# Hybrid DeltaNet/MLA trunk on one core: three products give [channel, token], and the stream's norm acts after the products that read it

## Chip, cores and metric

One NeuronCore of a Trainium2 chip runs the whole program. The metric is device time in microseconds (us) of one execution; lower is better.

## What is computed (the reference, cut)

A residual stream of 16 meta tokens and 1024 tokens, 1024 channels, goes through one gated-DeltaNet layer (A) and one multi-head latent attention layer (B). All is float32.

```python
o = gated_delta_rule(q, k, v, g, beta)               # A, 8 heads of 128
o = rms_norm(o, o_gain) * silu(gate)                 # per head
x = x + o @ w_out                                    # A's output projection
h = rms_norm(x, kv_norm);  c = h @ w_down            # 1024 -> 256 + 64
c_kv = rms_norm(c[..., :256], g_latent);  k_pe = c[..., 256:]
h = rms_norm(x, b_norm);  z = h @ w_in               # 1024 -> 384 + 1024
c_q = rms_norm(z[..., :384], g_q_latent);  gate = z[..., 384:]
o = attention(c_q, c_kv, k_pe) * silu(gate)
out = x + o @ w_out                                  # B's output projection, meta tokens dropped
```

## The kernel before, in words

Every float32 product is made of three F32R products, high by high, high by low and low by high (`mm3`, L92 to L95), so one 128x128 weight block costs three matmuls, each with its own weight load. A product over 1024 channels is 8 blocks (`kt`), 24 matmuls into one PSUM bank. The order of instructions on each engine is set by a scheduler at build time from the program's order, its pools and their buffer counts; at run time each engine works in that order and waits on semaphores. All loads and stores of the stages below are issued by SyncE (SP), one after the other.

Stages around the change, in time order. Tokens stand in chunks TOKC of 272, 384 and 384 columns, or in tiles (16 meta tokens, t = -1, and eight of 128).

- Gates of A (L739 to L754): per head three products of 24 matmuls, [channel, token], Silu on ScalarE (ACT). Gate 7 stays in SBUF as `glast`.
- Output projection of A (L758 to L853). `out_gather` loads a tile of o, scales it by the heads' norms (VectorE, L766), turns it with 8 transposes (L776), multiplies by the gate and splits it into oTh and oTl. `out_project` multiplies: oT is stationary, 512 columns of the weight move, twice 24 matmuls for a tile, result [token, channel]. The residual is added (L824), the row stored to x1_scr; Square with a running sum and an rsqrt give the norm, GpSimd (POOL) scales the row (xs, L830), and `turn` transposes it again (8 per tile, L840) into h1_hi and h1_lo, which are [channel, token] and normalised.
- Latents (L864 to L970): per tile 24 matmuls of 320 columns for the key side and 24 of 384 for the query side, [token, channel]; norms per row, then transposes (L940, L958) and a split into ckvT and cqT.
- Gate of B: per head 2 x 24 matmuls of 512 columns, and ACT takes Silu straight from PSUM (L84, called there). Then attention.
- Output projection of B (`out_b`): per tile a load of oT (512 KB), a cast and a subtraction, a load of x1, 2 x 24 matmuls of 512 columns (wf), an addition, one store of 512 KB.

PSUM banks in these stages have three names: sc (5 banks, products), bd (2, transposes and small products) and pt (1).

Of the kernel before, what the change touches and what calls it, by code (L numbers as in the profile page):

```python
# [121 lines left out]
def body(ctx: ExitStack, tc: tile.TileContext, I, out):  # L122
# [63 lines left out]
    with ExitStack() as la:  # L186
        hp = la.enter_context(tpool(name="hT", bufs=1, side="right"))
        wp = la.enter_context(tpool(name="wA", bufs=2, side="right"))
        zp = la.enter_context(tpool(name="zA", bufs=2, side="right"))
# [547 lines left out]
        with ExitStack() as lr:  # L737
            rp = lr.enter_context(tpool(name="wr", bufs=2))
            for h in range(H):  # L739
                hi, lo = weights(3 * D + h * P)  # L740
                z = zp.tile([P, 3 + L], F32, tag="z", name=nm("zg"))[:, 0:L] if h < HG else glast[:, h - HG, :]
                for c, (a, b) in enumerate(TOKC):
                    act(z[:, a:b], gemm_T(hi, lo, c), AF.Silu)
                if h < HG:
                    SY.dma_start(gt_scr[h * P:(h + 1) * P, :], z)
                raw = rp.tile([P, D], F32, tag="raw", name=nm("raw"))
                SY.dma_start(raw, I["a_w_out"][0, h * P:(h + 1) * P, :])
                last = split_w(raw, w_hi[:, h, :], w_lo[:, h, :], col("og"), A)
                if h > 1:
                    next(norms, None)  # L750
            for _ in norms:
                pass
            with tc.issue_after(last.ins):
                refine_norms()  # L754
# [751 lines left out]
```

## Time and profile before

| | |
|---|---|
| median of 3 runs | 1332.45 us (1331.79 to 1336.11) |
| profiled execution: time, span | 1339.67 us, 1338.0 us |
| TensorE (PE) busy | 1301.6 us, 97% of the span |
| VectorE (DVE), ScalarE (ACT), GpSimd (POOL) busy | 67%, 43%, 24% |
| mean granted TensorE clock | 0.986 |

The times come from a profile of one execution; its span is the time from the first to the last instruction. Busy times of matmuls overlap one another, since they are pipelined, so the price of a matmul is read from the distance of two starts in a row, not from its duration.

### The profile page before, as it was taken

What the parts mean: (1) busy time and instruction counts of PE and PEld (TensorE: products, weight loads), DVE (VectorE), ACT (ScalarE), POOL (GpSimd) and SP (SyncE); (2) the same over time, 40 slices, a digit from 0 to 9 for tenths busy, and PEclk for the clock granted to TensorE, in tenths of its full rate; (3) what the DMA queues carried; (4) which work ended last, traced back from release to release, by engine and by line L of the source; (5) the groups of instructions that cost most, each with busy time, mean ns of one, the idle gap of its engine ahead of it and who ended that gap; (6) DMA issues with size and microseconds to landing.
All of it is one profiled execution on the core that took longest, in us unless ns stands there. A gap on an engine that the chain in (4) does not pass through costs nothing.

```text
span 1338.0 us, 24787 instructions
## 1 busy us (share of the span) xinstructions
PE 1301.6 (97%) x9047; PEld 1181.1 (88%) x9047; DVE 893.4 (67%) x2588; ACT 581.4 (43%) x1760; POOL 327.2 (24%) x597
## 2 busy tenths in 40 slices
PE   6999999999999999999999999997999999998998
PEld 4889989989998999997887798886999999998886
DVE  7679779878976894652553855225888888787321
ACT  6543444344424431232132342116777777776200
POOL 3141121122111100040111402212534535447000
PEclk9999999999998999999999999999999999999999
DMA  5111112111111203164441303211101101014443
GB/s 195 32 34 49 49 30 60 36 41 42 54 48 31 58 27 97 60 229 134 154 134 66 94 1 112 95 48 61 55 25 40 51 25 33 22 36 147 137 142 110
DMA packets 91676, 96.80 MB, mean 72 GB/s; under 512 B 27423, under 2 KB 72415, under 8 KB 91555
## 3 DMA queue, kind: packets, MB, share of 16 engines
q1 hardware_dynamic: 91554, 95.23, 22.8%
q8 instruction: 71, 1.16, 0.4%
q14 instruction: 51, 0.41, 0.1%
HBM read 68.19 MB, written 27.01 MB: 71 GB/s over the span
## 4 chain that ended last, share of the span: by engine, by line
PE 83%; DVE 6%; ACT 3%; issue 3%; POOL 2%; DMA 1%; SPq 0%; DVEq 0%; POOLq 0%; ACTq 0%
PE mm L93 9%; PE mm L94 9%; PE mm L95 9%; PE sc L95 6%; PE sc L94 6%; PE sc L93 6%; PE bd L93 5%; PE bd L95 4%; PE bd L94 4%; PE pt L1336 2%; PE tr L507 2%; PE ch L639 1%; PE tr L499 1%; PE ch L649 1%; PE ch L635 1%
## 5 line engine op out<-in xcount | busy, mean ns | idle before, releaser
L93 PE MATMUL mm<-hT_hi,whi 128*128 128x384 f32 (+1 forms) x768 | 257.2, 335 | 4.3 <-ACT hT_hi L292 4.3
L94 PE MATMUL mm<-hT_lo,whi 128*128 128x384 f32 (+1 forms) x768 | 256.4, 334 | 0.5 <-DVE hT_lo L293 0.5
L95 PE MATMUL mm<-hT_hi,wlo 128*128 128x384 f32 (+1 forms) x768 | 255.9, 333 | 0.0
L93 PEld LDWEIGHTS mm<-hT_hi,whi 128*128 128x128 f32 x768 | 147.7, 192 | 6.3 <-POOL wab L100 5.0
L94 PEld LDWEIGHTS mm<-hT_lo,whi 128*128 128x128 f32 x768 | 147.7, 192 | 2.2 <-DVE hT_lo L293 1.0
L95 PEld LDWEIGHTS mm<-hT_hi,wlo 128*128 128x128 f32 x768 | 148.1, 193 | 1.1 <-issue 0.4
L100 POOL TENSOR_SCALAR whi<-raw 128x512 fp32r<-128x512 f32 x48 | 34.4, 733 | 171.4 <-PE mm L94 136.7
L113 DVE TENSOR_TENSOR pTl<-pt,pTh 128x256 fp32r<-128x256 f32 (+2 forms) x112 | 54.9, 494 | 10.2 <-ACT pTh L112 8.8
L395 ACT COPY z<-mm 128x384 f32<-128x384 f32 (+1 forms) x72 | 32.0, 445 | 65.4 <-PE mm L95 64.4
L84 ACT ACTIVATE P<-P,mx 128x144 f32<-128x144 f32 (+3 forms) x64 | 50.6, 791 | 21.9 <-DVE mx L1294 19.1
L93 PE MATMUL sc<-wo_hi,oTh 128*128 128x512 f32 (+1 forms) x144 | 57.5, 399 | 1.1 <-DVE oTl L783 1.1
L95 PE MATMUL sc<-wo_hi,oTl 128*128 128x512 f32 (+1 forms) x144 | 57.2, 397 | 0.0
L94 PE MATMUL sc<-wo_lo,oTh 128*128 128x512 f32 (+1 forms) x144 | 56.9, 395 | 0.0
L399 DVE SCALAR_TENSOR_TENSOR kn<-z,pcol,kn 128x384 f32<-128x384 f32 (+1 forms) x72 | 41.5, 576 | 22.9 <-ACT kn L397 22.1
L112 ACT CAST pTh<-pt 128x256 fp32r<-128x256 f32 (+2 forms) x112 | 47.3, 427 | 15.7 <-PE pt L1336 8.6
L101 DVE TENSOR_TENSOR wlo<-raw,whi 128x512 fp32r<-128x512 f32 x64 | 46.8, 741 | 8.4 <-POOL whi L100 8.3
L95 PE MATMUL sc<-h_hi,wlo 128*128 128x512 f32 x128 | 50.8, 397 | 0.0
L94 PE MATMUL sc<-h_lo,whi 128*128 128x512 f32 x128 | 50.6, 396 | 0.0
L1307 POOL TENSOR_SCALAR P<-P,sl 128x144 f32<-128x144 f32 (+3 forms) x64 | 49.7, 778 | 3.8
L93 PE MATMUL sc<-h_hi,whi 128*128 128x512 f32 x128 | 50.5, 395 | 0.0
L93 PE MATMUL sc<-kn_hi,qn_hi 128*128 128x272 f32 (+3 forms) x160 | 48.5, 305 | 2.0 <-DVE mx L1294 1.5
L107 DVE SCALAR_TENSOR_TENSOR wlo<-raw,pcol,whi 128x128 fp32r<-128x128 f32 x64 | 23.4, 429 | 39.9 <-POOL whi L106 39.9
(390 smaller groups left out, 3900.3 us busy)
## 6 DMA issues: line engine op xcount, KB each, us to landing
raw<-in_a_w_in SPq DMA_DIRECT2D x64, 256.0 KB
xt<-in_x SPq DMA_DIRECT2D x14, 512.0 KB
o_scr<-o SPq DMA_DIRECT2D x64, 64.0 KB
raw<-in_a_w_out SPq DMA_DIRECT2D x8, 512.0 KB
on<-o_scr SPq DMA_DIRECT2D x8, 512.0 KB
x_scr<-xt SPq DMA_DIRECT2D x8, 512.0 KB
raw<-in_b_w_in SPq DMA_DIRECT2D x8, 512.0 KB
gb_scr<-z SPq DMA_DIRECT2D x8, 512.0 KB
```

The source lines that it names most:

```text
L84: i = A.activation(out_ap, in_ap, func, **kw)
L93: TE.matmul(ps, ahi, bhi, start=first, stop=False)
L94: TE.matmul(ps, ahi, blo, start=False, stop=False)
L95: TE.matmul(ps, alo, bhi, start=False, stop=last)
L100: eng.tensor_scalar(out=hi, in0=raw, scalar1=1.0, scalar2=1.0, op0=ALU.mult, op1=ALU.mult)
L101: V.tensor_tensor(out=lo, in0=raw, in1=hi, op=ALU.subtract)
L112: A.copy(hi, ps)
L113: V.tensor_tensor(out=lo, in0=ps, in1=hi, op=ALU.subtract)
L395: A.copy(z[:, 3 + a:3 + b], gemm_T(hi, lo, c))
L399: V.scalar_tensor_tensor(out=yc, in0=z[:, a + j:b + j], scalar=col("cw", 24 * j + m), in1=yc, op0=ALU.mult, op1=ALU.add)
L507: TE.matmul(ps[:, P * j:P * j + P], kn[:, a:b], qT[:, a:b], start=True, stop=True)
L1307: G.tensor_scalar(out=Pm[:, 0:n], in0=Pm[:, 0:n], scalar1=s, scalar2=1.0, op0=ALU.mult, op1=ALU.mult)
```

## The change

Three products now have weights as the stationary operand and tokens as the moving one, so that their results come as [channel, token].

- A's output projection goes by chunks of tokens: 8 channel blocks of 24 matmuls for each chunk. The residual comes from x_r, a turned copy of the input; x1_scr holds [channel, token]. The sum is copied (ACT) and subtracted (DVE) straight into h1_hi and h1_lo, unnormalised; ACT squares it and DVE sums the squares over blocks into ssx. L830's scaling and `turn` are gone.
- `out_gather` scales by the heads' norms with 8 ACT multiplications in place of one on DVE. The gathers of tiles -1, 0 and 1 stand between the chunks of gate 7, the others between the channel blocks of chunks 0 and 1.
- Latents go by chunks: 3 blocks for the keys (128, 128, 64 rows) and 3 for the queries, left in PSUM until a norm is there. Norms come as rows repeated over all partitions: a float32 product with `ones` (L1009, L1039) sums squares over channels, then Ln, Exp and a step of refinement. The stream's norm is added into the latents' norms (vrow); where no norm follows it multiplies (rrow): the rotary keys and the gate of B, whose Silu then reads SBUF.
- B's output projection goes by chunks of 256, 512 and 256 tokens with 8 blocks each, loads and stores of 128 or 256 KB per block, and gives [channel, token]; the host turns the result.

The core of the diff (the functions of before stand above):

```diff
-    x1_scr = dram("x1_scr", [L, D])
+    x1_scr = dram("x1_scr", [D, L])
...
+        def out_gather(t, bank, oT_hi, oT_lo):
 
-            oT_hi = so.tile([P, KT, P], F32R, tag="oTh", name=nm("oTh"))
-            oT_lo = so.tile([P, KT, P], F32R, tag="oTl", name=nm("oTl"))
+            on, gtile = rows.pop(t)
+            for h in range(H):
+                x = on[:k, h * P:(h + 1) * P]
+                A.mul(x, x, ro[:k, s, h:h + 1])
...
-                A.copy(oT_hi[:, hs4, 0:k], gs)
-                V.tensor_tensor(out=oT_lo[:, hs4, 0:k], in0=gs, in1=oT_hi[:, hs4, 0:k], op=ALU.subtract)
-            return oT_hi, oT_lo
-        gathered = {t: out_gather(t, bank) for t in (-1, 0)}
+                A.copy(oT_hi[:, hs4], gs)
+                V.tensor_tensor(out=oT_lo[:, hs4], in0=gs, in1=oT_hi[:, hs4], op=ALU.subtract)
+        def gate(h, between=()):
+            hi, lo = weights(3 * D + h * P)
+            z = zp.tile([P, 3 + L], F32, tag="z", name=nm("zg"))[:, 0:L] if h < HG else glast[:, h - HG, :]
+            for c, (a, b) in enumerate(TOKC):
+                act(z[:, a:b], gemm_T(hi, lo, c), AF.Silu)
+                for f in between[c:c + 1]:
+                    f()
+            if h < HG:
...
+        gate(HG)
+        so = so_.enter_context(tpool(name="so", bufs=3))
+        W0 = TOKC[0][1]
+        oT0 = [so.tile([P, KT, W0], F32R, tag=y, name=y, bufs=1) for y in ("oT0h", "oT0l")]
+        def first_gather(t):
+            a, b = tok(t)
+            return lambda: out_gather(t, bank, *(x[:, :, a:b] for x in oT0))
+        for t in (-1, 0, 1):
+            gather_rows(t, so)
+        gate(H - 1, [first_gather(t) for t in (-1, 0, 1)])
...
+        def out_project(c, m, oT):
+            a, b = TOKC[c]
+            n = b - a
+            for k in range(m if m else 0, min(m + 2, KT - 1) + 1):
+                if (c, k) not in xts:
+                    load_xt(c, k)
+            xt = xts.pop((c, m))
+            ps = bank2("mm", [P, 512])[:, 0:n]
+            ms = slice(m * P, (m + 1) * P)
+            for kt in range(KT):
+                mm3(ps, w_hi[:, kt, ms], w_lo[:, kt, ms], oT[0][:, kt], oT[1][:, kt], kt == 0, kt == KT - 1)
+            V.tensor_tensor(out=xt, in0=ps, in1=xt, op=ALU.add)
+            SY.dma_start(x1_scr[ms, a:b], xt)
+            A.copy(h1_hi[:, m, a:b], xt)
+            V.tensor_tensor(out=h1_lo[:, m, a:b], in0=xt, in1=h1_hi[:, m, a:b], op=ALU.subtract)
+            if m == 0:
+                act(ssx[:, a:b], xt, AF.Square)
+            else:
+                sq = pools["x"].tile([P, n], F32, tag="sq", name=nm("sq"))
+                act(sq, xt, AF.Square)
+                V.tensor_tensor(out=ssx[:, a:b], in0=sq, in1=ssx[:, a:b], op=ALU.add)
...
+        oT = oT0
+        for c, (a, b) in enumerate(TOKC):
+            if c == 1:
+                so_.close()
+                last = so_.enter_context(tpool(name="so3", bufs=1))
+                pools["x"] = so_.enter_context(tpool(name="xo2", bufs=2))
+                oTl = [last.tile([P, KT, 384], F32R, name=y) for y in ("oTlh", "oTll")]
+            if c == 0:
+                nxt = [x[:, :, TOKC[2][0]:TOKC[2][1]] for x in (h1_hi, h1_lo)]
+            elif c == 1:
+                nxt = oTl
+            else:
+                lg_.close()
+                rrow = lpre.enter_context(tpool(name="rows", bufs=1, side="right")).tile([P, L], F32, name="rrow")
+                wdp = lwd.enter_context(tpool(name="wd", bufs=1, side="right"))
+                wd_hi, wd_lo = (wdp.tile([P, KT, WD], F32R, name=x) for x in ("wd_hi", "wd_lo"))
+                nxt = None
...
+                    t = 3 * c + 2 + m // 2
+                    x = slice(P * (m // 2), P * (m // 2 + 1))
+                    out_gather(t, bank2, *(y[:, :, x] for y in nxt))
+                    if t + 2 < NT:
+                        gather_rows(t + 2, sg)
+                if nxt is None:
+                    split_w(wdr[m], wd_hi[:, m, :], wd_lo[:, m, :], col("kv", m))
+                    if m + 2 < KT:
+                        fetch_wd(m + 2)
+            oT = nxt
...
+            def root(out_ap, put):
+                n = out_ap.shape[-1]
+                sh, t = (sp.tile([P, 384], F32, tag=x, name=nm(x), bufs=1)[:, 0:n] for x in ("rsh", "rt"))
+                y = out_ap
+                put(sh)
+                act(y, sh, AF.Ln, scale=-2.0)
+                act(y, y, AF.Exp, scale=-0.5)
+                V.tensor_tensor(out=t, in0=y, in1=y, op=ALU.mult)
+                V.tensor_tensor(out=t, in0=t, in1=sh, op=ALU.mult)
+                V.scalar_tensor_tensor(out=out_ap, in0=t, scalar=1.5, in1=y, op0=ALU.add, op1=ALU.mult)
+            def stream_norms(c):
+                a, b = TOKC[c]
+                ps = bank2("tb", [P, 512])[:, 0:b - a]
+                TE.matmul(ps, ones, ssx[:, a:b], start=True, stop=True)
+                V.tensor_scalar(out=vrow[:, a:b], in0=ps, scalar1=-0.5 * EPS / D, scalar2=-0.5 * EPS * EPS,
+                                op0=ALU.mult, op1=ALU.add)
+                root(rrow[:, a:b], lambda sh: V.tensor_scalar(
+                    out=sh, in0=ps, scalar1=-0.5 / D, scalar2=-0.5 * EPS, op0=ALU.mult, op1=ALU.add))
+            def block(hi, lo, m, k, a, b):
+                ps = bank2("mm", [P, 512])[0:k, 0:b - a]
+                ms = slice(m * P, m * P + k)
+                for kt in range(KT):
+                    mm3(ps, hi[:, kt, ms], lo[:, kt, ms], h1_hi[:, kt, a:b], h1_lo[:, kt, a:b],
                         kt == 0, kt == KT - 1)
...
+            def normalise(blocks, ss, a, b, width, hi, lo, to, gain):
+                n = b - a
+                ps = bank2("tb", [P, 512])[:, 0:n]
+                TE.matmul(ps, ones, ss, start=True, stop=True)
+                row = sp.tile([P, 384], F32, tag="row", name=nm("row"))[:, 0:n]
+                root(row, lambda sh: V.scalar_tensor_tensor(
+                    out=sh, in0=ps, scalar=-0.5 / width, in1=vrow[:, a:b], op0=ALU.mult, op1=ALU.add))
+                for j, x in enumerate(blocks):
+                    y = sp.tile([P, 384], F32, tag="nb", name=nm("nb"))[:, 0:n]
+                    V.tensor_tensor(out=y, in0=x, in1=row, op=ALU.mult)
+                    g = col(gain, j)
+                    A.mul(hi[:, j, to:to + n], y, g)
+                    V.scalar_tensor_tensor(out=lo[:, j, to:to + n], in0=y, scalar=g, in1=hi[:, j, to:to + n],
+                                           op0=ALU.mult, op1=ALU.subtract)
...
+            def latent_kv(c):
+                a, b = TOKC[c]
+                kvs, ss = [], None
                 for j in range(2):
...
+                    kvs.append(block(wd_hi, wd_lo, j, P, a, b))
+                    for _ in range(2 * c):
+                        next(wqs, None)
+                    ss = squares(kvs[j], ss)
+                    soon()
+                later.append(lambda: normalise(kvs, ss, a, b, KVR, ckvT_hi, ckvT_lo, a, "gl"))
+                if c + 1 < len(TOKC):
+                    later.append(lambda: stream_norms(c + 1))
+                ps = block(wd_hi, wd_lo, 2, ROPE, a, b)
+                for _ in range(2):
+                    next(wqs, None)
+                kp = sp.tile([ROPE, 384], F32, tag="kp", name=nm("kp"), bufs=1)[:, 0:b - a]
+                V.tensor_tensor(out=kp, in0=ps, in1=rrow[0:ROPE, a:b], op=ALU.mult)
+                soon()
+                if c == 0:
+                    later.append(all_tables)
+                later.append(lambda: rotary(c, kp))
+            def latent_q(c):
+                a, b = TOKC[c]
+                a = max(a, NM)
+                qs, ss = [], None
                 for j in range(3):
...
+                    qs.append(block(wq_hi, wq_lo, j, P, a, b))
+                    ss = squares(qs[j], ss)
+                    soon()
+                later.append(lambda: normalise(qs, ss, a, b, QR, cqT_hi, cqT_lo, a - NM, "gq"))
+            stream_norms(0)
+            latent_kv(0)
+            latent_kv(1)
+            latent_q(0)
+            latent_kv(2)
...
+            latent_q(1)
+            latent_q(2)
+            soon()
...
-                    act(z[:, c], ps, AF.Silu)
+                    V.tensor_tensor(out=z[:, c], in0=ps, in1=rrow[:, cc], op=ALU.mult)
+                    act(z[:, c], z[:, c], AF.Silu)
...
+        def out_rows(c, n, pool, raw_tag):
+            oT = [pool.tile([P, KT, n], F32R, tag=y, name=nm(y), bufs=1) for y in (f"oTh{c}", f"oTl{c}")]
+            k = D // n
+            for q in range(0, KT, k):
+                raw = pool.tile([P, D], F32, tag=raw_tag, name=nm("ro"), bufs=2).rearrange("p (k n) -> p k n", n=n)
+                SY.dma_start(raw, ot_scr[q * P:(q + k) * P, c:c + n].rearrange("(k p) n -> p k n", p=P))
+                A.copy(oT[0][:, q:q + k], raw)
+                V.tensor_tensor(out=oT[1][:, q:q + k], in0=raw, in1=oT[0][:, q:q + k], op=ALU.subtract)
+            return oT
+        def out_b(c, n, m, oT, pool, tag):
+            ms = slice(m * P, (m + 1) * P)
+            xt = pool.tile([P, D], F32, tag=tag, name=nm("xt"), bufs=2)[:, 0:n]
+            SY.dma_start(xt, x1_scr[ms, NM + c:NM + c + n])
+            ps = bank2("bd", [P, 512])[:, 0:n]
+            for kt in range(KT):
+                mm3(ps, w_hi[:, kt, ms], w_lo[:, kt, ms], oT[0][:, kt], oT[1][:, kt], kt == 0, kt == KT - 1)
+            V.tensor_tensor(out=xt, in0=ps, in1=xt, op=ALU.add)
+            SY.dma_start(out[ms, c:c + n], xt)
+        oT = out_rows(0, 256, wf, "raw")
+        for m in range(KT):
+            out_b(0, 256, m, oT, wf, "raw")
+    wl = lf.enter_context(tpool(name="wl", bufs=1))
+    oTs = {c: out_rows(c, n, wl, f"raw{c}") for c, n in ((256, 512), (768, 256))}
+    for c, n in ((256, 512), (768, 256)):
+        for m in range(KT):
+            out_b(c, n, m, oTs[c], wl, f"raw{c}")
```

On TensorE at the end of gate 7, before: mm is gate 7's last product, L776 are transposes of o for the meta tile and tile 0, sc_1220 is the first projection.

```order
L95 MATMUL mm_1203_7335<-hT_hi,wlo_1194_7190 128x384
L776 MATMUL tr_1209_7384<-ident,on_1205_7377 128x16 x4
L776 MATMUL tr_1210_7392<-ident,on_1205_7377 128x16 x4
L776 MATMUL tr_1215_7408<-ident,on_1211_7401 128x128 x4
L776 MATMUL tr_1216_7416<-ident,on_1211_7401 128x128 x4
L93 MATMUL sc_1220_7451<-wo_hi,oTh_1207_7382 16x512
L94 MATMUL sc_1220_7451<-wo_lo,oTh_1207_7382 16x512
L95 MATMUL sc_1220_7451<-wo_hi,oTl_1208_7383 16x512
```

After, the same place (L767 are the transposes of tile 1, oT0h and oT0l the gathered operand of chunk 0):

```order
L95 MATMUL mm_1213_7416<-hT_hi,wlo_1196_7210 128x384
L767 MATMUL tr_1214_7450<-ident,on_1205_7310 128x128 x4
L767 MATMUL tr_1215_7458<-ident,on_1205_7310 128x128 x4
L93 MATMUL sc_1223_7502<-oT0h,wo_hi 128x272
L93 MATMUL sc_1225_7534<-oT0h,wo_hi 128x272
L93 MATMUL sc_1232_7597<-oT0h,wo_hi 128x272
L93 MATMUL sc_1235_7631<-oT0h,wo_hi 128x272
L93 MATMUL sc_1242_7694<-oT0h,wo_hi 128x272
L94 MATMUL sc_1223_7502<-oT0l,wo_hi 128x272
L95 MATMUL sc_1223_7502<-oT0h,wo_lo 128x272
```

The transposes of the first two tiles left this place, tile 1's are there instead, and five blocks each start with one product that needs oT0h alone.

In the latents after, TensorE's end of the first key chunk: sc_1327 is its rotary block, sc_1340 the next chunk's first block, pt_1331 and pt_1337 are sums by `ones`.

```order
L95 MATMUL sc_1327_8631<-h_hi,wd_lo 64x272
L1039 MATMUL pt_1331_8666<-ssb_1324_8601,ones 128x272
L93 MATMUL sc_1340_8696<-h_hi,wd_hi 128x384
L94 MATMUL sc_1340_8696<-h_lo,wd_hi 128x384
L95 MATMUL sc_1340_8696<-h_hi,wd_lo 128x384
L93 MATMUL sc_1340_8696<-h_hi,wd_hi 128x384
L94 MATMUL sc_1340_8696<-h_lo,wd_hi 128x384
L1009 MATMUL pt_1337_8685<-ssx,ones 128x384
```

DVE at that place (kp, rsh, rt and row are the root of pt_1331; vrow and rsh_1338 read pt_1337; wq_lo splits weights):

```order
L1097 TENSOR_TENSOR kp_1330_8664<-sc_1327_8631,rrow 64x272
L1041 SCALAR_TENSOR_TENSOR rsh_1333_8669<-pt_1331_8666,vrow 128x272
L107 SCALAR_TENSOR_TENSOR wq_lo<-rq_1319_8562,pcol,wq_hi 128x384
L971 TENSOR_SCALAR qS<-qS 128x512
L965 TENSOR_TENSOR sinS<-sinS,gr 128x9x32
L1001 TENSOR_TENSOR rt_1334_8670<-row_1332_8668 128x272
L1011 TENSOR_SCALAR vrow<-pt_1337_8685 128x384
L1002 TENSOR_TENSOR rt_1334_8670<-rt_1334_8670,rsh_1333_8669 128x272
L107 SCALAR_TENSOR_TENSOR wq_lo<-rq_1328_8658,pcol,wq_hi 128x384
L1003 SCALAR_TENSOR_TENSOR row_1332_8668<-rt_1334_8670,row_1332_8668 128x272
L1013 TENSOR_SCALAR rsh_1338_8688<-pt_1337_8685 128x384
```

pt_1331 and pt_1337 use the one pt bank in turn, and the reader of pt_1331 (rsh_1333) stands behind kp; nothing of this was there before.

On SP around the start of B's output projection, before (raw holds oT or x1 of a tile, gt is attention's last output):

```order
L1442 DMA raw_2883_15613<-ot_scr 128x8x128
L1367 DMA ot_scr<-gt_2849_15444 128x256
L1444 DMA raw_2884_15615<-x_scr 128x1024
L1442 DMA raw_2889_15674<-ot_scr 128x8x128
L1444 DMA raw_2890_15676<-x_scr 128x1024
L1367 DMA ot_scr<-gt_2868_15541 128x256
L1454 DMA out<-raw_2884_15615 128x1024
L1442 DMA raw_2895_15735<-ot_scr 128x8x128
L1444 DMA raw_2896_15737<-x_scr 128x1024
```

After (ro is raw oT, xt the residual of one block):

```order
L1521 DMA ot_scr<-gt_2780_15548 128x256
L1598 DMA ro_2817_15869<-ot_scr 128x2x512
L1598 DMA ro_2818_15873<-ot_scr 128x2x512
L1598 DMA ro_2823_15887<-ot_scr 128x4x256
L1611 DMA out<-xt_2799_15630 128x256
L1598 DMA ro_2824_15891<-ot_scr 128x4x256
L1611 DMA out<-xt_2801_15659 128x256
L1598 DMA ro_2819_15877<-ot_scr 128x2x512
L1606 DMA xt_2803_15688<-x_scr 128x256
L1598 DMA ro_2820_15881<-ot_scr 128x2x512
L1606 DMA xt_2805_15717<-x_scr 128x256
```

Four more loads of 512 KB now stand ahead of xt_2803, the residual of the third block.

## Rows read from the trace of the kernel before

**Rows 1.** The page, part 1, busy time of TensorE.
```profile
PE 1301.6 (97%) x9047; PEld 1181.1 (88%) x9047; DVE 893.4 (67%) x2588; ACT 581.4 (43%) x1760; POOL 327.2 (24%) x597
```

**Rows 2.** Windows by stage: length, busy us (instructions) of PE, PEld, DVE, ACT, POOL; PEclk.
```profile
618.20:620.90 2.70, 1.63 (x17) 1.37 (x17) 1.98 (x8) 2.62 (x6) 0.00 (x0) 1.00 0.49 106
620.90:734.50 113.60, 113.57 (x548) 88.14 (x548) 52.97 (x110) 26.46 (x62) 11.66 (x9) 1.00 0.42 137
734.50:814.20 79.70, 76.40 (x461) 68.23 (x460) 54.33 (x199) 31.43 (x128) 14.92 (x25) 1.00 0.14 41
814.20:905.20 91.00, 90.25 (x388) 72.29 (x387) 28.30 (x81) 13.22 (x25) 24.19 (x59) 1.00 0.29 94
1243.70:1338.00 94.30, 89.40 (x398) 73.32 (x396) 22.33 (x28) 8.42 (x11) 0.00 (x0) 0.99 0.40 129
```

**Rows 3.** Timeline, TensorE: 512 columns, the first and last of five starts (projection).
```profile
689.57 0.39 PE L95 MATMUL sc<-wo_hi,oTl 128*128 128x512 f32 x1
...
690.50 0.39 PE L93 MATMUL sc<-wo_hi,oTh 128*128 128x512 f32 x1
```

**Rows 4.** Timeline, TensorE: 384 columns, first and last of six starts (a gate).
```profile
599.70 0.33 PE L93 MATMUL mm<-hT_hi,whi 128*128 128x384 f32 x1
...
600.58 0.34 PE L95 MATMUL mm<-hT_hi,wlo 128*128 128x384 f32 x1
```

**Rows 5.** Timeline, TensorE: 272, then 256 columns (attention): first, sixth and tenth start.
```profile
1119.74 0.29 PE L93 MATMUL sc<-kn_hi,qn_hi 128*128 128x272 f32 x1
...
1120.37 0.28 PE L93 MATMUL sc<-kn_hi,qn_hi 128*128 128x256 f32 x1
...
1120.84 0.28 PE L1290 MATMUL sc<-kr,qr_lo 128*128 128x256 f32 x1
```

**Rows 6.** Timeline, TensorE: transposes of 128 columns between two projections.
```profile
709.06 0.60 PE L840 MATMUL pt<-ident,xs 128*128 128x128 f32 x4
709.50 1.04 PE L776 MATMUL bd<-ident,on 128*128 128x128 f32 x8
```

**Rows 7.** Timeline, TensorE, start of the kernel: `ones` products, later 272-column ones.
```profile
5.48 1.11 PE L280 MATMUL tr<-part,ones 128*128 128x272 f32 x2
...
5.48 1.57 PE L280 MATMUL tr<-part,ones 128*128 128x272 f32 x3
...
17.93 0.39 PE L95 MATMUL mm<-hT_hi,wlo 128*128 128x272 f32 x1
18.15 0.29 PE L93 MATMUL mm<-hT_hi,whi 128*128 128x272 f32 x1
18.28 0.29 PE L94 MATMUL mm<-hT_lo,whi 128*128 128x272 f32 x1
```

**Rows 8.** Timeline, all engines: gate 7 ends, the projection begins.
```profile
620.05 1.43 ACT L782 CAST oTh<-gtile 128x64 fp32r<-128x64 f32 x4
...
620.93 0.39 PE L93 MATMUL sc<-wo_hi,oTh 128*16 128x512 f32 x1 [1.10 <-DVE oTl L783]
```

**Rows 9.** Groups of ScalarE: busy us, mean ns (projection; latents).
```profile
L782 ACT CAST oTh<-gtile 128x512 fp32r<-128x512 f32 x16 | 9.7, 613 | 0.9 <-DVE gtile L781 0.9
...
L115 ACT ACTIVATE cqT<-bd,pcol 128x128 fp32r<-128x128 f32 x22 | 8.1, 367 | 16.8 <-PE bd L958 13.6 <-DVE cqT L116 3.2
```

**Rows 10.** Groups of VectorE in the latents.
```profile
L107 DVE SCALAR_TENSOR_TENSOR wq_lo<-rq,pcol,wq_hi 128x384 fp32r<-128x384 f32 x8 | 5.5, 728 | 1.9 <-POOL wq_hi L106 1.9
```

**Rows 11.** Timeline, TensorE: waits in the latents.
```profile
751.13 0.44 PE L94 MATMUL sc<-wq_lo,h_hi 128*128 128x384 f32 x1 [0.67 <-DVE wq_lo L107]
```

**Rows 12.** Groups of weight loads: the page, part 5.
```profile
L93 PEld LDWEIGHTS mm<-hT_hi,whi 128*128 128x128 f32 x768 | 147.7, 192 | 6.3 <-POOL wab L100 5.0
```

**Rows 13.** The chain of waits: start us, us, what (attention's end).
```profile
1207.92 1.70 DMA ot_scr<-gt
...
1220.05 3.79 DMA raw<-in_b_w_out
```

**Rows 14.** Timeline: the last instruction of the kernel.
```profile
1333.86 0.34 SPq L1454 DMA_DIRECT2D out<-raw  x1
```

More of the change, by code (lines that the diff above doesn't have):

```diff
@@ L736, in body @@
         glast = wo.tile([P, H - HG, L], F32, name="glast")
[L737 to L754, printed above, removed]
@@ L833, in turn @@
-        def turn(t, xs):
-            a, b = tok(t)
-            k = b - a
-            for half in range(2):
-                ps = bank2("tb", [P, 4, P])
-                for j in range(4):
-                    kt = 4 * half + j
-                    TE.transpose(ps[:, j, 0:k], xs[:k, kt * P:(kt + 1) * P], ident[:k, :k])
-                hs4 = slice(4 * half, 4 * half + 4)
-                split_ps(ps[:, :, 0:k], h1_hi[:, hs4, a:b], h1_lo[:, hs4, a:b])
-        done, xts = {}, {-1: load_xt(-1)}
@@ L845, in body @@
-        for t in range(-1, NT + 2):
-            if t + 1 < NT:
-                xts[t + 1] = load_xt(t + 1)
-            if 0 < t < NT:
-                gathered[t] = out_gather(t, bank2)
-            if -1 <= t - 1 < NT:
-                done[t - 1] = out_project(t - 1, *gathered.pop(t - 1))
-            if -1 <= t - 2:
-                turn(t - 2, done.pop(t - 2))
-        lo_.close()
+        ssx = lpre.enter_context(tpool(name="ssx", bufs=1, side="right")).tile([P, L], F32, name="ssx")
+        pools = {"x": so_.enter_context(tpool(name="xo", bufs=2))}
@@ L963, in body, with fetch_wq @@
-            for t in range(-1, NT + 1):
-                if t < NT:
-                    latent_kv(t)
-                if t > 0:
-                    latent_q(t - 1)
-                if t == 3:
-                    wg0 = load_wg(lpre.enter_context(tpool(name="wg0", bufs=1, side="right")), 0)
+            wqr = []
+            def fetch_wq(kt):
+                wqr.append(sp.tile([P, WQ], F32, tag="rq", name=nm("rq"), bufs=3))
+                SY.dma_start(wqr[kt], I["b_w_in"][0, kt * P:(kt + 1) * P, 0:QR])
@@ new lines, in block, with squares @@
+            def block(hi, lo, m, k, a, b):
[3 more added lines that the diff above has]
+                    mm3(ps, hi[:, kt, ms], lo[:, kt, ms], h1_hi[:, kt, a:b], h1_lo[:, kt, a:b],
+                        kt == 0, kt == KT - 1)
+                return ps
+            def squares(ps, ss):
+                n = ps.shape[-1]
+                if ss is None:
+                    ss = sp.tile([P, 384], F32, tag="ssb", name=nm("ssb"))[:, 0:n]
+                    act(ss, ps, AF.Square)
+                    return ss
+                sq = sp.tile([P, 384], F32, tag="sqb", name=nm("sqb"))[:, 0:n]
+                act(sq, ps, AF.Square)
+                V.tensor_tensor(out=ss, in0=sq, in1=ss, op=ALU.add)
+                return ss
```

218 lines of the change are left out of this document (105 added, 113 removed).

## The prediction

> **What bounds the kernel now.** I read the page first: TensorE (PE) is busy for 97% of the span [rows 1], so time is saved only where PE's own work or its idle time shrinks. Then the windows by stage [rows 2]: PE is idle for 0.03 us of 113.6 in A's output projection, 3.3 of 79.7 in the latents, 0.8 of 91.0 in the gate of B and 4.9 of 94.3 in B's output projection. Then the timeline, for the price of one matmul, from start to start: 512 columns take 0.93/4 = 0.232 us [rows 3], 384 take 0.88/5 = 0.176 [rows 4], 272 take 0.63/5 = 0.126 and 256 take 0.47/4 = 0.118 [rows 5], a transpose 0.44/4 = 0.11 [rows 6]. That is 0.45 to 0.46 ns for a column whatever the width, so what counts is columns.
>
> **A's output projection.** Before, nine tiles of 48 matmuls are 432 x 0.232 = 100.2 us, and the meta tile's 16 rows cost as much as 128. After, 192 matmuls of 272 and 384 of 384 columns are 24.2 + 67.6 = 91.8: 8.4 less. `turn` goes: 64 wide transposes and 8 narrow ones, 7.4 us (the last tile's ran inside the latents' window). From gate 7's end to the end of the projection it was 2.7 + 113.6 = 116.3 us [rows 2]. After, the meta tile's and tile 0's transposes run inside gate 7, which ends 1.4 later; tile 1's transposes follow (0.9), then a wait, 91.8, and six gathers of 0.88 (5.3). The wait was 1.10, for gate 7's last Silu, four casts of 1.43 together on ACT and DVE's oTl [rows 8]. In the new order five blocks can start as soon as tile 1's casts are there, so I take 1.7 (bounds 0 and 3). Sum 101.1, **-15.2**.
>
> What must keep up here: in chunk 0, two blocks and a gather are 48 x 0.126 + 0.88 = 6.9 us of PE. ACT then has 8 multiplications at 0.367, two casts at 0.613 [rows 9] and four copies and squares of 272 columns, some 0.42 each between those two prices: 5.9. DVE has six operations on 272 columns and five of a gather; by 0.728 for 384 columns [rows 10], an upper price, 0.52 each and 3.9: 7.0. Both fit or nearly, and five banks lie between; 0, bounds 0 and 4.
>
> **Latents and gate of B.** The key side was 216 matmuls of 320 columns, at 0.46 ns a column 31.8; after it is 72 x (0.126 + 0.176 + 0.176) = 34.4, as the 64 rotary channels cost a whole block. The query side stays: 192 x 0.176 = 33.8 before, and after 72 x (0.118 + 0.176 + 0.176) = 33.8. The 40 wide transposes of latents (4.4) and the rest of `turn` (1.5) go, nine small ones for the rotary key come (0.9). New are nine float32 products with `ones`, 3104 columns. One such record takes the difference of two rows, 0.46 us, where an F32R product of the same 272 columns takes 0.22, and there are two records to a product; where that F32R product takes 0.13 [rows 7], I scale 0.92 to 0.92 x 0.126/0.22 = 0.53. The granted clock reads 1.00 at both places, but the steps are those of the two levels, 1.2 and 2.4 GHz: no long work stood before the slow ones. PE hardly pauses in the latents, so I take the faster level: 1.95 ns a column, 6.0 us; at the slower one it would be 10.5.
>
> Columns before: 31.8 + 33.8 + 4.4 + 1.5 = 71.5, in a window of 79.7: 8.2 went to waits, named as POOL's and DVE's weight splits [rows 11]. After: 75.1. The key weights are split during the projection, so their waits go; new ones come. By the changed program's order DVE has 129 instructions here, 58 of them on 384 columns; at up to 0.728 for those [rows 10] and in proportion for the others that is 65 to 78 us of the 75, where it had 54.3 [rows 2]. It is in order, and the one pt bank passes from pt_1331 to pt_1337 only when DVE has read it: behind kp and two weight splits a product waits one or two DVE operations. Three such places, 1 us each: 3 (bounds 0 and 9, as before). 78.1 against 79.7: **-1.6**. The gate's products are the same 384; the multiplication moved to DVE stands last in place of nothing, a 512-column operation near the 0.613 of a cast [rows 9]: **+0.3**. Attention has the same matmuls: 0, bounds ±1.5.
>
> **B's output projection.** 384 x 0.232 = 89.1 before; after, 192 x (0.118 + 0.232 + 0.118) = 89.9: +0.8. At its start the loads for the later chunks stand in SP's queue ahead of the third block's residual, xt_2803. The store of the second block goes out at 2 x 2.83 + 0.4 = 6.1, two issues (0.34 each [rows 14]) make 6.8, and 128 KB behind a 512 KB load land 3.79 + 1.70 later [rows 13], 12.3; with the addition 12.7. The fifth block needs that bank at 4 x 2.83 = 11.3: 1.4 late, and the sixth by the next 512 KB load again some 1.7: +3.1 (bounds 0 and 8). At the end a store of 128 KB lands in place of 512 KB, 1.70 for 3.79 at most: I take -1.3, bounds 0 and -2.1. Together **+2.6**.
>
> Later each residual tile is reloaded through two buffers: add (0.4), issue, store, issue, load. With 1.70 for store and for load this is 4.5 of the 5.66 us that two blocks of 256 columns last, so 0. [...] No row here shows such a load by itself.
>
> **Sum.** -15.2 - 1.6 + 0.3 + 2.6 = -13.9. The profiled execution took 1339.67 for a span of 1338.0; it would take 1325.8. The median lies 7.2 under the profiled time, so 1332.45 - 13.9 = **1318.6**.
>
> **Rivals.** (1) The forecast, 1318.6, from 1312 to 1325 with its own bounds: 0.62. (2) Nothing waits: latents -3, B's projection -3.1 and the tail's other 0.8, the first wait -1.7: 1310. For it, five banks and many of these waits were short before: 0.15. (3) DVE becomes the bound of the latents: their waits are 9 instead of 3, and the `ones` products cost 10.5 instead of 6.0, B's start 8 instead of 3.1: -13.9 + 15.4 = +1.5 at the worst; with half of it, 1326: 0.16. (4) Narrow matmuls are paced by their weight loads. A load takes 192 ns [rows 12], longer than a product of 272 or 256 columns steps. If it showed, 264 products of 272 columns would each cost 0.066 more and 456 of 256 columns 0.074 more: 17.4 + 33.7, 1370, slower; it decides from 14 us of it on, 0.02 for each of the 720 products. Against it: attention's 256-column products, each with its own load, step by 0.118 [rows 5], and those of 384 columns by 0.176, both under a load's time. The Trainium skill ("TensorE: Matmul & The Clock Gate", back-to-back issue gap) has both instructions set the pace, 81 ns at 128 columns and 131 at 512; by that the projection would go from 432 x 0.131 = 56.6 to about 63, up by 6. The rows show 0.232 and 0.118, in proportion: 0.03. (5) The buffer loop above binds in B's projection: above a landing of 2.3 us it costs 6 x (2 landings - 4.58), three turns in each chunk of 256 columns; at 3.5 the 14 us are gone, and at 3.8 it adds 18.1: 1337, slower. 512 KB landed in 3.79, but 128 KB in 1.70 [rows 13]: 0.04.
>
> **Range and chances.** About 0.3% (4 us) is what a measurement can tell from no change. Cases 1 and 2 are faster wholly, 3 mostly (0.13). Faster 0.90, same 0.05, slower 0.05. The range takes in case 2's 1310 and the middle of 3: 1309 to 1327.
>
> **What would show it.** Right: matmuls of the projection step 0.126 and 0.176 with no idle time, and gate 7's end to its end is near 101 us; from there to the gate of B some 78; B's projection near 97, with its idle time in the first eight blocks; `ones` records near 0.27 us for 272 columns. Wrong: idle time of PE put down to DVE in the latents above 6 us, to DMA behind xt in the last 90 us, or 272-column steps near 0.19.

## The result and the profile after

The changed kernel takes 1325.62 us (median of 13 executions, 1320.71 to 1330.71) where the kernel before, run beside it, takes 1334.40 (13, 1331.28 to 1338.49): ratio 0.9932, 95% interval 0.9915 to 0.9949, that is 8.8 us less. Run again later, the same kernel gave 0.9925 (0.9896 to 0.9954). The forecast was 13.9 us less, range 1309 to 1327: the way and the range hold, the gain is somewhat under two thirds of what was forecast.

The profiled executions differ by more: spans of 1338.0 and 1320.9 us, 17.1 apart. The page and one window, 300 to 450 us from the start, of the changed kernel:

```profile
PE 1281.3 (97%) x9320; PEld 1196.2 (91%) x9320; DVE 901.6 (68%) x2534; ACT 598.3 (45%) x1764; POOL 320.0 (24%) x588
300.00:450.00 150.00, 149.32 (x1231) 1.00 0.17 46
```

and the same window of the kernel before:

```profile
300.00:450.00 150.00, 149.31 (x1176) 0.94 0.17 44
```

(length, PE busy, PEclk, DMA share, GB/s). In the same 150 us, at a granted clock of 1.00 instead of 0.94, the changed kernel got 55 more matmuls done, in a part of the program that the change leaves alone. So I compare from gate 7's end on, where the granted clock is 0.98 or above in every stage of both. Windows by stage of the changed kernel (columns as in [rows 2]):

```profile
610.60:613.10 2.50, 0.89 (x9) 0.65 (x6) 1.35 (x3) 2.42 (x4) 0.00 (x0) 1.00 0.65 213
613.10:710.30 97.20, 97.18 (x624) 97.02 (x625) 52.91 (x106) 41.24 (x107) 5.91 (x8) 1.00 0.48 147
710.30:788.20 77.90, 76.84 (x460) 70.24 (x459) 49.87 (x117) 22.93 (x62) 11.76 (x16) 1.00 0.13 38
788.20:881.70 93.50, 91.16 (x394) 73.01 (x393) 38.78 (x86) 14.01 (x22) 24.12 (x59) 1.00 0.27 91
881.70:1221.50 339.80, 325.16 (x2571) 315.77 (x2570) 268.66 (x867) 249.40 (x802) 163.91 (x305) 0.99 0.16 51
1221.50:1320.90 99.40, 93.14 (x590) 85.08 (x588) 23.02 (x36) 7.66 (x9) 0.00 (x0) 0.98 0.39 123
```

Against [rows 2], projection with its lead-in: 116.3 to 99.7; latents 79.7 to 77.9; gate of B with its last Silu 91.0 to 93.5; attention 338.5 to 339.8; B's projection 94.3 to 99.4. From gate 7's end 719.8 became 710.3, and 1.4 us of transposes moved ahead of that point: 8.1 less, which agrees with the medians. The gain was made where it was forecast and in its size; the last three stages added 8.9 us, where the forecast had 2.9.

The projection runs as forecast. TensorE's timeline: its one wait, the first and last of eleven starts at 272 columns, and of nine at 384 columns:

```profile
613.12 0.65 PE L93 MATMUL sc<-oT0h,wo_hi 128*128 128x272 f32 x3 [1.63 <-ACT oT0h L773]
...
614.83 0.29 PE L95 MATMUL sc<-oT0h,wo_lo 128*128 128x272 f32 x1
...
616.09 0.29 PE L93 MATMUL sc<-oT0h,wo_hi 128*128 128x272 f32 x1
...
689.76 0.34 PE L93 MATMUL sc<-oTlh,wo_hi 128*128 128x384 f32 x1
...
691.17 0.34 PE L95 MATMUL sc<-oTlh,wo_lo 128*128 128x384 f32 x1
```

Ten steps make 1.26 us and eight 1.41, 0.126 and 0.176 each.

The first two losses are waits of TensorE in the gate of B:

```profile
799.76 0.40 PE L95 MATMUL sc<-h_hi,wlo 128*128 128x512 f32 x1
801.37 0.50 PE L93 MATMUL sc<-h_hi,whi 128*128 128x512 f32 x1 [1.21 <-POOL whi L106]
801.71 0.40 PE L94 MATMUL sc<-h_lo,whi 128*128 128x512 f32 x1
803.23 0.51 PE L95 MATMUL sc<-h_hi,wlo 128*128 128x512 f32 x1 [1.13 <-DVE wlo L107]
```

These are the second head's weights, whi and wlo, which POOL and DVE split. POOL's timeline shows what stood ahead of whi:

```profile
794.66 0.62 POOL L100 TENSOR_SCALAR uvh<-uvr 128x512 fp32r<-128x512 f32 x1
798.52 1.16 POOL L100 TENSOR_SCALAR uqh<-uqr 128x1152 fp32r<-128x1152 f32 x1 [3.25 <-DMA uqr<-in_b_w_uq]
800.22 3.95 POOL L106 TENSOR_SCALAR whi<-raw,pcol 128x128 fp32r<-128x128 f32 x8 [0.53 <-PE sc L95]
```

POOL sat 3.25 us on uqr, a weight that only attention needs. SP issued the three attention weights from 791.09 on, 2.9 us after the gate's first product (788.17); in the kernel before it was 814.44 against 814.21, and POOL began whi at 823.73, 1.6 us ahead of the second head. What SP waited for ahead of these loads, its longest wait around the gate's start, was the first operation of the latents' last norm (rsh, on DVE; us in total, times, longest):

```profile
SPq L1141 <- DVE rsh L1041: 30.4, 1, 30.4
```

In the kernel before it was the last product of the latents. That the loads wait for the last norm to leave its buffers is my reading of this; no run tests it alone.

The second wait, for wlo, has a cause of its own on DVE:

```profile
799.72 1.36 DVE L101 TENSOR_TENSOR uql<-uqr,uqh 128x1152 fp32r<-128x1152 f32 x1 [1.78 <-POOL uqh L100]
801.00 0.72 DVE L1048 SCALAR_TENSOR_TENSOR cqT<-nb,pcol,cqT 128x384 fp32r<-128x384 f32 x1
801.64 1.28 DVE L1166 TENSOR_TENSOR z<-sc,rrow 128x512 f32<-128x512 f32 x2
802.84 1.47 DVE L107 SCALAR_TENSOR_TENSOR wlo<-raw,pcol,whi 128x128 fp32r<-128x128 f32 x4
```

The split of wlo stands behind uql, which had waited for POOL, the end of the last norm (cqT) and the first head's two multiplications by rrow (z), 1.28 us that the change itself moved to DVE. TensorE had read the first block of whi at 801.37; wlo began at 802.84. By the timeline, without the two multiplications wlo could have begun 1.2 us earlier, about as long as the wait; this is an estimate that no run tests alone.

The third loss is a wait of 3.03 us in B's projection, and what follows it:

```profile
1237.40 0.28 PE L95 MATMUL bd<-oTh,wf_lo 128*128 128x256 f32 x1
1240.71 0.39 PE L93 MATMUL bd<-oTh,wf_hi 128*128 128x256 f32 x1 [3.03 <-DVE xt L1610]
...
1241.40 0.28 PE L95 MATMUL bd<-oTh,wf_lo 128*128 128x256 f32 x1
1241.52 0.28 PE L93 MATMUL bd<-oTh,wf_hi 128*128 128x256 f32 x1
...
1242.13 0.42 PE L94 MATMUL bd<-oTl,wf_hi 128*128 128x256 f32 x1
1242.34 0.41 PE L95 MATMUL bd<-oTh,wf_lo 128*128 128x256 f32 x1
```

```profile
1241.90:1245.10 3.20, 3.20 (x17) 0.50 0.62 167
```

For a microsecond after the wait the steps are 0.12 us, then for 3.2 us 0.21, at a granted clock of 0.50. The block that begins there took 4.41 us in place of 2.88, so the wait of 3.03 cost 4.6. DVE's and SP's timelines, the wait followed back:

```profile
1240.23 0.42 DVE L1610 TENSOR_TENSOR xt<-bd,xt 128x256 f32<-128x256 f32 x1 [0.76 <-DMA xt<-x_scr]
```

```profile
1235.10 0.36 SPq L1598 DMA_DIRECT2D ro<-ot_scr  x1
1235.82 0.33 SPq L1606 DMA_DIRECT2D xt<-x_scr  x1
```

The addition that frees the bank had no residual yet. Its load, xt_2803, went out at 1235.82 and landed 4.4 us later, because SP stood before it at the load of ro_2819 until DVE had split ro_2817.

### The profile page after: what moved, and what is told of

It is laid out like the page before. It is cut to its first block, busy times and chain, and to the rows that moved or that the text cites. A ratio compares the mean times of both kernels' runs of the same rounds, so it can differ in the third digit from the quotient of the medians.

```text
span 1320.9 us, 25401 instructions
## 1 busy us (share of the span) xinstructions
PE 1281.3 (97%) x9320; PEld 1196.2 (91%) x9320; DVE 901.6 (68%) x2534; ACT 598.3 (45%) x1764; POOL 320.0 (24%) x588
## 5 line engine op out<-in xcount | busy, mean ns | idle before, releaser
L93 PE MATMUL bd<-oTh,wf_hi 128*128 128x256 f32 (+1 forms) x192 | 61.4, 323 | 3.0 <-DVE xt L1610 3.0
L95 PE MATMUL bd<-oTh,wf_lo 128*128 128x256 f32 (+1 forms) x192 | 61.8, 322 | 0.0
L94 PE MATMUL bd<-oTl,wf_hi 128*128 128x256 f32 (+1 forms) x192 | 61.7, 322 | 0.0
L1610 DVE TENSOR_TENSOR xt<-bd,xt 128x256 f32<-128x256 f32 (+1 forms) x24 | 12.3, 514 | 67.9 <-PE bd L95 59.9
L1461 POOL TENSOR_SCALAR P<-P,sl 128x144 f32<-128x144 f32 (+3 forms) x64 | 52.4, 820 | 4.1
L400 DVE SCALAR_TENSOR_TENSOR kn<-z,pcol,kn 128x384 f32<-128x384 f32 (+1 forms) x72 | 42.1, 585 | 15.2 <-ACT kn L398 14.3
```

Of the source, the lines that this page charges most:

```text
L93: TE.matmul(ps, ahi, bhi, start=first, stop=False)
L94: TE.matmul(ps, ahi, blo, start=False, stop=False)
L95: TE.matmul(ps, alo, bhi, start=False, stop=last)
L400: V.scalar_tensor_tensor(out=yc, in0=z[:, a + j:b + j], scalar=col("cw", 24 * j + m), in1=yc, op0=ALU.mult, op1=ALU.add)
L1461: G.tensor_scalar(out=Pm[:, 0:n], in0=Pm[:, 0:n], scalar1=s, scalar2=1.0, op0=ALU.mult, op1=ALU.mult)
```

## Experiments

Stage lengths below are read from the traces, from a first start to a last end. In the executions that share a stage's code the projection repeats within 0.04 us and the latents within 0.5, while gate 7's end, after code that no edit but gath_after touches, moves between 610.6 and 618.2. So a stage tells more than a median of a few runs. For the changed kernel the projection is 99.90 us from gate 7's end, and the latents from there to the gate's first product 77.65; the 99.7 and 77.8 of the expectations below put the projection's end one matmul early.

**wg_first** and **xt_pack** undo one loss each, **both** the two together. In wg_first the second head's weights are loaded (SP) and split (POOL) ahead of the three attention weights:

```diff
...
+            hold = []
+            wg1 = load_wg(wg, 1, hold)
+            wts = {0: []}
+            w0 = pair_weights(0, wts[0])
+            with tc.issue_after(hold[0].ins):
+                next(w0)
...
-                    next(w0, None)
+                    with tc.issue_after(hold[-1].ins):
+                        next(w0, None)
```

> The changed kernel with one order altered: the second head's gate weights are loaded and split before the three pair weights of attention (uk, uv, uq) on SP and POOL. Theory 1 (the gate of B lost 2.3 us because POOL's split stands behind a weight that landed late): the two waits of 1.21 and 1.13 us at the second head go, the stretch of the gate's products falls from 92.4 to about 90.1 us, and the whole by about 2.3 us against the changed kernel. Rival (the split is late because its own load is late, whatever stands ahead): both waits stay, within 0.5 us.

Measured: 1325.67 us, ratio 0.9922 (0.9896 to 0.9949). TensorE's timeline and the window of the gate of B:

```profile
805.76 0.50 PE L95 MATMUL sc<-h_hi,wlo 128*128 128x512 f32 x1 [0.58 <-DVE wlo L943]
792.70:884.20 91.50, 90.92 (x394) 73.22 (x394) 39.49 (x86) 13.94 (x22) 24.41 (x59) 1.00 0.29 93
```

Of the two waits one is left, 0.58 us for DVE's half of the split; from the start of the gate's first product to that of its last it is 90.5 us in place of 92.5. Theory 1 holds for the wait on POOL: the split was late for what stood ahead of it. The edit moves the load on SP and the split on POOL together, so it does not tell which of the two queues held it; in old_out, below, which has the gate's old order, POOL waited a further 1.40 us for raw, the split's own load, after it had split uqr. The wait that is left is DVE's: the same two multiplications by rrow (1.51 us) stand just ahead of wlo, whose whi had been begun 8.6 us before. In the median 2 us do not show: the ratio is at most 0.001 under the changed kernel's, well inside both intervals.

```diff
...
+        packs = {}
...
-            xt = pool.tile([P, D], F32, tag=tag, name=nm("xt"), bufs=2)[:, 0:n]
-            SY.dma_start(xt, x1_scr[ms, NM + c:NM + c + n])
+            k = D // n
+            if m % k == 0:
+                packs[c] = pool.tile([P, D], F32, tag=tag, name=nm("xt"), bufs=2).rearrange("p (k n) -> p k n", n=n)
+                SY.dma_start(packs[c], x1_scr[m * P:(m + k) * P, NM + c:NM + c + n].rearrange("(k p) n -> p k n", p=P))
+            xt = packs[c][:, m % k, :]
```

> The changed kernel with the residual of B's projection loaded for several blocks at once (512 KB a load: four blocks of 256 columns or two of 512), through the same two buffers. Theory 1 (the sixth block waited 3.03 us for a residual queued on SP behind loads of later chunks, and the slower steps that follow, 1.5 us, come from that wait): the wait and the slow steps both go, B's projection is shorter by about 4.5 us, and so is the whole. Rival (the loads of the later chunks keep the transfers busy, and the wait turns into one for oT of the second chunk): the wait moves to the ninth block, at least 2 us of it stay.

Measured: 1326.21 us, ratio 0.9926 (0.9902 to 0.9951). B's projection to the end of the span:

```profile
1231.30:1325.80 94.50, 91.31 (x590) 83.49 (x588) 22.58 (x36) 7.61 (x8) 0.00 (x0) 1.00 0.40 130
```

94.5 us in place of 99.4, granted clock 1.00, no wait above 0.6 in it: the wait and the slower steps went together, 4.9 us, and did not come back as a wait for oT. The median shows nothing of it. In part that may be the granted clock: over the six executions it was 0.983 to 0.988, over the thirteen of the changed kernel 0.985 to 0.995. In this trace gate 7 ended at 618.0 us, with 0.94 granted between 300 and 450 us, and after the two waits in the gate of B, still there, the steps of 512 columns rose to 0.43 us for 3 us, which they had not done in the first profile.

> Both edits together in the changed kernel. Theory 1: the savings add up, 2.3 + 4.5 = 6.8 us under the changed kernel, near 1319 us of time where the changed kernel has 1325.6, ratio to before near 0.988. Rival (the waits are slack that the next stage takes back): no more than 3 us.

Measured: 1322.29 us, ratio 0.9891 (0.9864 to 0.9918); gate 90.5, B's projection to the end 94.3. Beside the changed kernel on one chip it was run again:

> The changed kernel once more, as the measure for the next. Theory 1: projection 99.7 us from gate 7's end, latents 77.8, the gate's two waits and the 3 us wait of the sixth block are there again, whatever the granted clock does in the first 600 us. Rival (the waits of the first profile were chance): at least one of the three is under 0.3 us.

> Both edits (gate weights of the second head first; residuals loaded four blocks at once) again, beside the changed kernel on one chip. Theory 1: 4 to 7 us under it, 0.3 to 0.5%. Rival (what the first call showed was the granted clock): within 2 us.

Measured: after_again 1327.91 us, 0.9925; both_again 1320.58 us, 0.9874 (0.9845 to 0.9904): 7.3 us less, 0.5%, and each of its six executions was faster than each of the seven of after_again. The waits of the changed kernel were all there again (1.10 in the latents, 0.48 and 1.13 in the gate, 3.79 in B's projection). Stage by stage, after_again, then both_again (gate; B's projection to the end):

```profile
790.30:883.10 92.80, 91.19 (x394) 73.05 (x393) 38.79 (x86) 14.02 (x22) 24.06 (x59) 1.00 0.28 92
1222.10:1322.00 99.90, 92.91 (x590) 85.01 (x588) 22.79 (x36) 7.61 (x8) 0.00 (x0) 0.98 0.39 123
```

```profile
793.90:885.40 91.50, 90.92 (x394) 73.10 (x393) 39.50 (x86) 13.94 (x22) 24.35 (x59) 1.00 0.29 93
1224.90:1319.40 94.50, 91.28 (x590) 83.49 (x588) 22.52 (x36) 7.61 (x8) 0.00 (x0) 1.00 0.40 130
```

1.3 and 5.4, 6.7 together: the savings add up, and this version beats both kernels.

All traces say the same. The gate, from its first product's start to its last's, took 91.7 to 96.1 us in the seven with the changed order, against 90.5 in each of the three with wg_first's; B's projection to the end took 99.3 to 101.1 in six with loads by block, against 94.3 to 94.6 in the three with xt_pack's.

**old_out** puts the old projection of B into the changed kernel: `out_b` of before, with x1_scr and the output taken as flat memory of the old shape.

> The changed kernel with B's output projection as before (tiles of tokens, 512 columns moving, one 512 KB load of oT and one of the residual per tile, one store of 512 KB). The residual is read from the same store as if it were [token, channel], and the result is written as if it were [channel, token], so that values are out of place; work and traffic are those of before. Theory 1 (the new projection of B costs 4 to 5 us more than the old one, in its first six blocks): 4 to 5 us under the changed kernel, with no wait above 1 us in the projection. Rival (chunks by themselves do not cost anything, the rise of the last stretch is the granted clock of that execution): within 1.5 us of the changed kernel.

Measured: 1322.29 us, ratio 0.9897 (0.9869 to 0.9925).

```profile
1226.80:1319.80 93.00, 88.63 (x398) 73.27 (x396) 21.67 (x28) 7.68 (x9) 0.00 (x0) 1.00 0.39 132
```

93.0 us against 99.4: the chunked projection costs 6.4 us, 4.9 of it the wait with its slower steps (xt_pack), 1.5 columns and the rest. Against the trace of the kernel before, whose old projection took 94.3, it was 5.1.

**meta3** and **turn2** test the two halves of the projection's gain in the kernel before.

```diff
-                for kt in range(KT):
+                for kt in range(KT if t >= 0 else 1):
...
```

> The kernel before, with the meta tile's output projection cut to the first of its eight weight blocks: 6 matmuls in place of 48, so the 16 meta rows of the stream are wrong. Theory 1 (a matmul costs its moving columns, so 16 rows cost as much as 128; half of the projection's gain in the changed kernel is this): 42 x 0.232 = 9.7 us off the projection, 116.05 to 106.3 us from gate 7's end. Rival (a matmul of 16 rows costs less, and the gain came from elsewhere): under 3 us.

```diff
                     TE.transpose(ps[:, j, 0:k], xs[:k, kt * P:(kt + 1) * P], ident[:k, :k])
+                    TE.transpose(ps[:, j, 0:k], xs[:k, kt * P:(kt + 1) * P], ident[:k, :k])
```

> The kernel before, with each transposition of the normalised stream (`turn`, 72 of them) issued twice into the same place. Theory 1 (these transposes lie on TensorE's own path, which is what their removal gave back): 64 x 0.11 and 8 short ones, about 7.4 us more from gate 7's end to the gate of B. Rival (TensorE has slack around them that hides them): under 2 us.

From gate 7's end to the projection's last matmul, 116.05 before; meta3:

```profile
614.20:720.60 106.40, 105.30 (x521) 85.24 (x521) 54.02 (x116) 29.61 (x66) 11.34 (x9) 1.00 0.45 149
```

From start to end that is 106.31: 9.74 off, as worked out, while the medians differ by 11.6 us (ratio 0.9914, 0.9885 to 0.9943). turn2, projection and latents:

```profile
617.30:739.30 122.00, 120.90 (x618) 95.07 (x619) 56.83 (x116) 28.04 (x66) 10.24 (x9) 1.00 0.39 130
739.30:821.50 82.20, 78.78 (x480) 69.95 (x479) 53.96 (x199) 32.06 (x129) 16.28 (x25) 1.00 0.13 39
```

121.97 and 82.23 for 116.05 and 79.95: 8.2 more (12.0 by the medians, ratio 1.0079, 1.0049 to 1.011). Both halves lay on TensorE's path in full.

**ones2**:

```diff
                 TE.matmul(ps, ones, ssx[:, a:b], start=True, stop=True)
+                TE.matmul(ps, ones, ssx[:, a:b], start=True, stop=True)
...
                 TE.matmul(ps, ones, ss, start=True, stop=True)
+                TE.matmul(ps, ones, ss, start=True, stop=True)
```

> The changed kernel with each of the nine float32 products with `ones` of the latents issued twice into the same bank. Theory 1 (a product costs 1.68 ns a column, as the next F32R matmul's late start shows, not the 0.03 us between its two records): 3104 x 1.68 = 5.2 us more between the projection's end and the gate of B. Rival A (the price is what the records show, 0.9 ns a column): 2.8 us. Rival B (VectorE sets the pace of the latents): under 1 us.

```profile
714.90:797.80 82.90, 81.33 (x474) 73.13 (x473) 50.02 (x117) 22.86 (x62) 11.91 (x16) 1.00 0.12 36
```

82.77 for 77.65: 5.1, ratio 0.997 (0.9943 to 0.9997). Eight of the nine doubled products lie in this stretch, 2720 columns; the ninth comes after the gate's first product. The price can be read from the first pair:

```profile
714.88 0.62 PE L1009 MATMUL pt<-ssx,ones 128*128 128x272 f32 x2
715.34 0.62 PE L1010 MATMUL pt<-ssx,ones 128*128 128x272 f32 x2
```

The second product starts 0.46 us after the first, 1.69 ns a column, and the pairs of 384 columns come to the same. At 1.68 the eight cost 4.6; the other 0.5 is waits, 0.81 and 0.71 us here for one of 0.96. So the price is theory 1's, and TensorE, not DVE, sets the pace of the latents. (The 0.03 us of the expectation lies between a product's second record and the next matmul, not between its two records.)

**norm_late**:

```diff
-                if c + 1 < len(TOKC):
-                    later.append(lambda: stream_norms(c + 1))
...
                     soon()
+                    if c > 0 and j == 0:
+                        stream_norms(c)
```

> The changed kernel with the second and third chunk's stream norms emitted after the first latent block of their chunk, so that the product with `ones` comes later in TensorE's order. Theory 1 (the 0.96 us wait in the latents is the single pt bank, read late by a VectorE in order): that wait goes, latents 1.0 us shorter, 76.9 in place of 77.8. Rival (VectorE is the bound of the latents, so the wait only moves): 77.8 within 0.2, with another wait of about 1 us later.

Measured: ratio 0.9967 (0.9945 to 0.9989), latents 79.79, 2.1 more. TensorE's timeline and a window:

```profile
736.78 0.27 PE L1060 MATMUL bd<-ident,kp 64*128 64x64 f32 x1 [1.65 <-ACT junk L84]
...
738.19 0.53 PE L93 MATMUL sc<-h_hi,wd_hi 128*128 128x384 f32 x1
738.51 0.53 PE L94 MATMUL sc<-h_lo,wd_hi 128*128 128x384 f32 x1
```

```profile
737.50:740.40 2.90, 2.90 (x10) 2.90 (x10) 2.90 (x12) 1.05 (x2) 1.00 (x2) 0.50 0.00 0
```

The wait for the pt bank went, but a transpose of the rotary key, now scheduled between two matmuls of a block, waited 1.65 us for ACT, and the next matmuls of 384 columns stepped by 0.32 instead of 0.176. Neither theory had this: the place of that transpose in the order is a second thing that the edit moved.

**gath_after**:

```diff
-        gate(H - 1, [first_gather(t) for t in (-1, 0, 1)])
+        gate(H - 1)
+        for t in (-1, 0, 1):
+            first_gather(t)()
```

> The changed kernel with the first three gathers behind gate 7 in place of between its chunks. In the order on ACT their scalings stay ahead of gate 7's end; the transposes and casts of the meta tile and tile 0 move behind it. Theory 1 (most of the projection's gain is columns and `turn`, and the placing only sets the first wait): gate 7 ends 1.4 us earlier, projection from its end 102 to 104 us in place of 99.7, total +0.5 to +3. Rival (the placing of the gathers carries the gain): over +5 us.

Measured: 103.10 us from gate 7's end, 3.2 more, of which 1.4 are the moved transposes and the rest longer waits. So the placing carries 1.8 us in the projection, as theory 1 has it. But the median, 1332.17 (ratio 0.9968, 0.9946 to 0.999), is 4.3 us over after_again's, above theory 1's +3. In this trace the gate of B took 96.1 us where after_again's took 91.8, in code that this edit leaves alone: the wait for whi was 2.17 in place of 0.48, and after it a dozen steps of 512 columns took 0.43 us, at a granted clock of 0.50:

```profile
810.00:814.60 4.60, 4.60 (x11) 3.62 (x12) 4.60 (x15) 0.13 (x1) 3.73 (x10) 0.50 0.47 166
```

The granted clock of the ten executions was 0.982 to 0.988, that of after_again's 0.988 to 0.994. Whether the edit has a part in that is open.

## Why the prediction was right, and its gain too large

- **Projection, -15.2.** Measured 116.05 to 99.90, less 1.4 moved: -14.7. The steps were 0.126 and 0.176 and the one wait 1.63 (1.7 taken). meta3 and turn2 show the two halves: 16 rows cost like 128, and `turn` lay on the path. The bound that ACT and DVE might hold it up was not needed, TensorE idled 0.02 us of 97.2.
- **Latents, -1.6.** Measured 79.95 to 77.65, -2.3. Two sizes in it were off. The `ones` products cost 1.68 ns a column, not 1.95: 5.2 us, not 6.0, of which 0.6 fell into the gate. And DVE was busy for 49.9 us, not 65 to 78: its operations on 384 columns that read SBUF or PSUM took 0.55 to 0.63, not the 0.728 of a weight split. The one wait was 0.96, at the pt bank as foreseen, for 3 taken. Columns, eight products and the wait make 74.6 of the 77.65; the other 3.0 lie in small steps that I did not take apart.
- **Gate of B, +0.3.** Measured +2.5, the step that failed: I costed only the moved multiplication, as one that "stands last in place of nothing", and took the weights' way as before. The latents' last norm now ends behind the gate's first products, the loads of attention's weights went out later with it, and POOL, which works in the order of its program, came to the second head's split only behind them (wg_first took this wait away). On DVE the first head's multiplications do not stand last either, but ahead of that split's other half. I had asked what stands behind a waiting instruction on DVE and SP, and not on POOL, nor on DVE in the gate.
- **Attention, 0.** Measured +1.2; from the gate's last product to B's first, kernels with the old front of this stage took 339.6 to 342.0 us, those with the new one 340.1 to 344.8, the shortest at a granted clock of 0.99 and the longest at 0.98. The difference starts with TensorE waiting 2.56 and 1.16 us for kk where it waited 1.31 and 1.65, with slower steps behind. Its cause stays open.
- **B's projection, +2.6.** Measured +5.2. The mechanism was right, SP's queue ahead of xt_2803; the size was not. The wait was 3.03 (3.1 taken), but for another reason of detail: there are three bd banks here, not two, so the sixth block waited, and the load left SP at 14.3 us after the projection's start, not at 6.8, since ro_2819 waited for a split. The 1.5 us of slower steps had no term. The columns cost 2.5, not 0.8, because 512 columns step by 0.227 in this stage and 256 by 0.120. The tail gave 1.65 (1.3 taken).
- **Rivals.** Narrow matmuls paced by their weight loads: refuted, 272 columns stepped by 0.126 with the load engine busy for 97.02 of 97.2 us. The buffer loop: after the sixth block no wait above 0.3, so 128 KB transfers were not its bound. DVE as the bound of the latents: refuted by ones2. What cut the gain is nearest to the third rival, by other waits.
- **The range.** Its upper end was the middle of the third rival, DVE as the bound of the latents, which did not come true. That 1325.62 lies inside, 1.4 us from that end, is in part luck: the range left room for losses, but not for these.

## What to carry to other kernels

Where a matmul costs its moving columns, ask which operand holds the padding: 16 rows as the stationary side were a full tile, as 16 more moving columns nearly nothing. When a stage gets a later end, follow everything that waits for its buffers, loads above all, through each in-order queue to the next stage, and ask of an operation that moves to another engine what stands behind it there. And compare stages, not spans, when the granted clock of an untouched stretch differs between two executions.
